# Moving a head's gate and its norm's last product from GpSimd to VectorE, read out of PSUM

## The chip, the cores and the metric

One core of one Trainium2 chip runs the whole model. The metric is the device time of one execution in microseconds; lower is better. The engines' names are those of the profile: PE is TensorE's matmuls (PEld its weight loads), DVE VectorE, ACT ScalarE, POOL GpSimd, SP SyncE, which here only issues DMAs.

## The reference

Two layers on 1024 rows of width 1024: an S5 layer, then a layer of differential attention with 8 heads, then a final norm. The change lies in the second layer:

```python
q, z = jnp.split(xn @ in_w, [QK_WIDTH], axis=-1)
...
o = diff_attention(q1, q2, k1, k2, v, lam)
o = rmsnorm(o, subln_g, SUBLN_EPS) * (1.0 - lam_init)
o = o.reshape(bsz, seq, ATTN_WIDTH) * jax.nn.silu(z)
return o @ out_w
```

Each head has 128 value columns. Its mixture o is normalized over these 128 (the gains are folded into weights) and multiplied by the gate silu(z). All products on TensorE are made from a high and a low part of one or both operands (three matmuls, lines 159 to 161).

## The kernel before

The S5 layer takes the first 485 us or so and is not touched. `layer1` walks over 32 steps: 8 heads, 4 blocks of 256 queries each, in falling order for odd heads. Everything lies transposed: 128 value columns on the partitions, 256 queries along the free axis. One step consists of

- `scores`: TensorE's products of k and q into a bank `s` (840, 841; the second multiplies a zero-padded tile `z00` to `z11`, which holds the high part of q for one of the two maps), VectorE's masked minimum (846), ACT's exponentials (848), and the difference of the two softmaxes (856);
- `turn`: TensorE transposes it into a bank `t` (874), ACT and VectorE split it into `ph` and `pl` (876, 877);
- `mix`: TensorE sums v times these into another bank `t` (890 to 892). ACT copies the bank to `ob` (896) and squares it twice (897, 898), GpSimd takes the low part of the squares (899);
- `head_norm`, one step later: two products with a matrix of ones add the squares over the partitions into a bank `t` (907, 908); ACT takes Ln and Exp (909, 910: the inverse root), into the tile `sq`; SP loads the gate `zt` from `zg` in HBM (913); GpSimd multiplies `ob` by `zt` (914) and by `sq` (915); the result goes to HBM (917), or for the last head into `oh` and `ol` by ACT and VectorE (919, 920).

The pool of the banks `t` has two buffers, shared by `turn`, `mix` and `head_norm`. TensorE's filler between the steps of one head are the projections of the next head's k, q, gate and v (`PLAN`): a head's q (lines 766 to 787) is rotated by VectorE (`xr`), cast by ACT into the padded tile (782, 783) and brought to `q` by SP (784, 785). At the last head the filler is the output projection of the first 512 columns (`out1`), and then `final`, which does the rest in four pieces of 256 columns. Their weights are loaded by SP into `mraw` (745) and split by ACT (`mhi` or `vh`, 749) and VectorE (`mlo` or `vl`, 750). The first weight that `final` loads into its own pool lies in memory that the attention layer's tiles give back, so its load waits for their last readers.

No order is written out for these engines: a list scheduler puts each engine's instructions into one fixed order, from its own costs, when the kernel is built. Each engine then runs its list in order and waits at an instruction for what that one needs. So a change of a few lines can move instructions in the whole layer.

Of the kernel before, what the change touches and what calls it, by code (L numbers as in the profile page):

```python
# [8 lines left out]
F32 = mybir.dt.float32  # L9
# [3 lines left out]
AF = mybir.ActivationFunctionType  # L13
# [5 lines left out]
P = 128  # L19
# [31 lines left out]
def rd(ap):  # L51
    return ap.bitcast(F32)


class Trunk:
# [822 lines left out]
            out.append((ph, pl))  # L878
        return out

    def mix(self, pt, v, qb):

        mm = self.nc.tensor.matmul
        o = self.pst.tile([P, 512], F32, name="t")
        nj = 2 * qb + 2
        for j in range(nj):
            c0 = 1 if j == nj - 1 else 0
            ov = o[:, c0 * P:2 * P]
            ph, pl = (t[:, j % 2, c0:2, :].rearrange("p a b -> p (a b)") for t in pt[j // 2])
            mm(ov, v[0][:, j, :], ph, start=j == 0, stop=False)  # L890
            mm(ov, v[0][:, j, :], pl, start=False, stop=False)  # L891
            mm(ov, v[1][:, j, :], ph, start=False, stop=j == nj - 1)  # L892
        ob = self.op.tile([P, 256], F32, name="ob")
        sq = self.op.tile([P, 256], F32, name="sq", bufs=1)
        sh, sl = (self.op.tile([P, 256], F32R, name=f"sq{x}", bufs=1) for x in "hl")
        self.nc.scalar.copy(ob, o[:, 0:256])
        self.nc.scalar.activation(sq, o[:, 0:256], AF.Square)
        self.nc.scalar.activation(sh, o[:, 0:256], AF.Square)
        self.nc.gpsimd.tensor_sub(sl, sq, rd(sh))
        return ob, sq, sh, sl  # L900

    def head_norm(self, ob, sq, sh, sl, zg, dst, qb):

        nc = self.nc
        V, S = nc.vector, nc.scalar
        ss = self.pst.tile([P, 512], F32, name="t")
        nc.tensor.matmul(ss[:, 0:256], self.onesr.broadcast_to([P, P]), sh, start=True, stop=False)
        nc.tensor.matmul(ss[:, 0:256], self.onesr.broadcast_to([P, P]), sl, start=False, stop=True)
        S.activation(sq, ss[:, 0:256], AF.Ln, bias=self.small1[:, 2:3], scale=1.0 / P)
        S.activation(sq, sq, AF.Exp, scale=-0.5)  # L910
        qs = slice(qb * 256, qb * 256 + 256)
        zt = self.op.tile([P, 256], F32, name="zt", bufs=1)
        nc.sync.dma_start(zt, zg[:, qs])
        nc.gpsimd.tensor_mul(ob, ob, zt)
        nc.gpsimd.tensor_mul(ob, ob, sq)  # L915
        if len(dst) == 1:
            nc.sync.dma_start(dst[0][:, qs], ob)
        else:
            S.copy(dst[0][:, qs], ob)
            V.tensor_sub(dst[1][:, qs], ob, rd(dst[0][:, qs]))  # L920

    def layer1(self, dbg=None):
        tc, nc, I = self.tc, self.nc, self.I
        V, G, S = nc.vector, nc.gpsimd, nc.scalar
        zg = [self.dr.tile([P, SEQ], F32, name="zg") for _ in range(NH)]
        og = [self.dr.tile([P, SEQ], F32, name="og") for _ in range(NH)]
        self.close_mm()
        with ExitStack() as es:
            pool = lambda n, b, **k: es.enter_context(tc.tile_pool(name=n, bufs=b, reuse_waits="tile", **k))
            rp = self.rp.enter_context(tc.tile_pool(name="rope", bufs=1, reuse_waits="tile"))  # L930
            self.RC = rp.tile([P, SEQ], F32, name="RC")
            self.RS = rp.tile([P, SEQ], F32, name="RS")
            self.xs = [rp.tile([P, 512], F32, name=f"xs{i}") for i in range(2)]
            nc.sync.dma_start(self.RC, I["rc"])
            nc.sync.dma_start(self.RS, I["rs"])
            for c in (0, 512):
                cs = slice(c, c + 512)
                V.tensor_mul(self.RC[:, cs], self.RC[:, cs], self.R1[:, cs])
                G.tensor_mul(self.RS[:, cs], self.RS[:, cs], self.R1[:, cs])
            for x in self.xs:  # L940
                G.memset(x, 0.0)
            self.vp = self.rp.enter_context(tc.tile_pool(name="vp", bufs=3, reuse_waits="tile"))
            self.tq, self.st, self.qp = pool("tq", 2), pool("st", 2), pool("qp", 2)
            zp = pool("zp", 1)
            self.padded = [[zp.tile([P, 512], F32R, name=f"z{i}{j}") for j in range(2)] for i in range(2)]
            for z in self.padded:
                for x in z:
                    G.memset(x.bitcast(F32), 0.0)
            self.ep, self.pp, self.op, self.tiny = pool("ep", 2), pool("pp", 4), pool("op", 2), pool("tiny", 4)
            self.pst, self.pss = pool("pst", 2, space=PSUM), pool("pss", 2, space=PSUM)  # L950
            self.psm = self.rp.enter_context(tc.tile_pool(name="psm", bufs=2, space=PSUM, side="right",
                                                          reuse_waits="tile"))
            vs, kq = {}, {}

            units = {
                "k": lambda h: kq.setdefault(h, []).append(self.project_kq(h, I["kv_w"], self.sm("gkv"), "k")),
                "q": lambda h: kq[h].append(self.project_kq(h, I["b_in_w"], self.gq, "q")),
                "v": lambda h: vs.update(zip((h, h + 1), self.project_v(h // 2))) if h % 2 == 0 else None,
                "g": lambda h: self.gate(h, zg[h]),
            }  # L960
            wv = self.load_v(0)
            wk = self.load_early(I["kv_w"], 0, self.sm("gkv"))
            vs.update(zip((0, 1), self.project_v(0, wv)))
            kq[0] = [self.project_kq(0, I["kv_w"], None, "k", wk)]
            units["q"](0)
            steps = [(h, 3 - qb if h in DESCENDING else qb) for h in range(NH) for qb in range(4)]
            nxt = self.scores(*kq[0], steps[0][1])
            self.gate(0, zg[0])
            norm = None
            for n, (h, qb) in enumerate(steps):  # L970
                cur = nxt
                if n + 1 < len(steps):
                    hn, qn = steps[n + 1]
                    nxt = self.scores(*kq[hn], qn)
                if h + 1 < NH:
                    for u in PLAN[n % 4]:
                        units[u](h + 1)
                pt = self.turn(cur, qb)
                if norm:
                    self.head_norm(*norm)  # L980
                if (h, n % 4) == (NH - 1, 0):
                    oh, ol = ([self.act(f"{x}{k}") for k in range(KT)] for x in ("oh", "ol"))
                    for k in range(NH - 1):
                        self.gated(og[k], EARLY, oh[k], ol[k])
                dst = (og[h],) if h < NH - 1 else (oh[h], ol[h])
                norm = (*self.mix(pt, vs[h], qb), zg[h], dst, qb)
            self.head_norm(*norm)
            parts = self.out1(og, oh, ol)
        self.final(oh, ol, *parts)
        self.rp.close()  # L990
# [188 lines left out]
```

## Time and profile before

| | us |
| --- | --- |
| runs, median (lowest to highest of 3) | 1091.48 (1090.79 to 1091.61) |
| profiled execution | 1093.5 |
| its span | 1091.7 |
| PE busy | 1061.9 |
| DVE busy | 822.5 |
| ACT busy | 623.9 |
| POOL busy | 235.3 |

The span is what the profiler recorded from the first instruction to the last; the execution's own time is a little longer. Busy time of an engine is the time in which one of its instructions ran. Times in a trace are microseconds from the start of the span.

### The profile page before, as it was taken

To read this page: it belongs to the slowest core of one execution; us is meant where nothing else is said; L and a number is where in the kernel's file an instruction comes from. 1 tells how busy PE (TensorE), PEld (TensorE's weight loads), DVE (VectorE), ACT (ScalarE), POOL (GpSimd) and SP (SyncE) were. 2 spreads that over 40 slices of the span, in tenths; PEclk is the share of its full clock that TensorE was granted. 3 is DMA by queue.
4 is the path that set the end of the run, shared out by engine and by line. 5 is a ranking of instruction groups with operands and counts; after the bars stand their busy time and mean duration, and the time that the engine had idled before them with its cause. 6 is when DMAs were issued, how large, how long until landed. Compare 5 with 4: busy or idle time off the path is not lost. (4 is left out here: it accounts for less than half of the span.)

```text
span 1091.7 us, 17715 instructions
## 1 busy us (share of the span) xinstructions
PE 1061.9 (97%) x6308; PEld 908.2 (83%) x6308; DVE 822.5 (75%) x1617; ACT 623.9 (57%) x1396; POOL 235.3 (22%) x237
## 2 busy tenths in 40 slices
PE   7999999999999999999999999999999999899996
PEld 5678888887788888998888898889988898788896
DVE  7789999984577543547898778877698777987475
ACT  6432343332534332436787788767788778785463
POOL 0000000000356112211222122221222222210258
PEclk9999999999899999999999999999999999999998
DMA  8143546544654445313122212222222222553344
GB/s 283 45 136 116 174 151 174 159 151 133 238 193 135 127 140 157 135 42 90 44 85 57 73 56 66 86 56 78 66 53 79 60 84 61 148 175 105 109 134 159
DMA packets 143143, 125.94 MB, mean 115 GB/s; under 512 B 9808, under 2 KB 123216, under 8 KB 143056
## 3 DMA queue, kind: packets, MB, share of 16 engines
q1 hardware_dynamic: 134736, 120.63, 36.0%
q10 hardware_dynamic: 8320, 4.19, 1.3%
q8 instruction: 49, 0.80, 0.3%
q14 instruction: 38, 0.31, 0.1%
HBM read 85.48 MB, written 33.03 MB: 109 GB/s over the span
## 5 line engine op out<-in xcount | busy, mean ns | idle before, releaser
L159 PE MATMUL pm<-h1h,mhi 128*128 128x512 f32 x352 | 139.5, 396 | 1.0 <-DVE xr L767 1.0
L160 PE MATMUL pm<-h1l,mhi 128*128 128x512 f32 x352 | 138.8, 394 | 0.0
L161 PE MATMUL pm<-h1h,mlo 128*128 128x512 f32 x352 | 138.6, 394 | 0.0
L848 ACT ACTIVATE e<-e,tiny 128x256 f32<-128x256 f32 (+7 forms) x128 | 99.3, 777 | 33.6 <-DVE tiny L846 32.5
L846 DVE CUSTOM_DVE_ANT_0 e<-s,tri 128x256 f32<-128x256 f32 (+7 forms) x128 | 94.8, 750 | 11.9 <-PE s L841 6.3
L750 DVE TENSOR_TENSOR mlo<-mraw,mhi 128x1024 fp32r<-128x1024 f32 (+1 forms) x44 | 59.9, 1360 | 42.7 <-ACT mhi L749 42.5
L749 ACT CAST mhi<-mraw 128x1024 fp32r<-128x1024 f32 (+1 forms) x44 | 45.3, 1030 | 76.0 <-PE ps L160 55.0
L159 PE MATMUL ps<-xh,mhi 128*128 128x512 f32 x208 | 82.2, 395 | 1.9 <-DVE evo L491 1.9
L161 PE MATMUL ps<-xh,mlo 128*128 128x512 f32 x208 | 81.9, 394 | 0.0
L160 PE MATMUL ps<-xl,mhi 128*128 128x512 f32 x208 | 81.7, 393 | 0.0
L159 PEld LDWEIGHTS pm<-h1h,mhi 128*128 128x128 f32 x352 | 66.2, 188 | 14.7 <-DVE xr L767 2.4
L161 PEld LDWEIGHTS pm<-h1h,mlo 128*128 128x128 f32 x352 | 66.2, 188 | 12.7
L771 POOL TENSOR_TENSOR xs<-xs,RS 128x512 f32<-128x512 f32 x32 | 42.9, 1340 | 156.0 <-DMA xs<-ze 114.2
L160 PEld LDWEIGHTS pm<-h1l,mhi 128*128 128x128 f32 x352 | 66.2, 188 | 12.2
L840 PE MATMUL s<-k,q 128*128 128x384 f32 (+4 forms) x192 | 67.9, 356 | 3.0 <-DMA q<-z 3.0
L915 POOL TENSOR_TENSOR ob<-ob,sq 128x256 f32<-128x256 f32 x32 | 25.7, 803 | 190.3 <-ACT sq L910 177.9
L841 PE MATMUL s<-k,z 128*128 128x384 f32 (+4 forms) x192 | 65.9, 346 | 0.0
L810 PE MATMUL pm<-mhi,h1h 128*128 128x256 f32 x224 | 64.5, 288 | 1.1 <-DVE z L698 0.8
L735 ACT ACTIVATE mhi<-mraw,small 128x128 fp32r<-128x128 f32 (+1 forms) x152 | 51.8, 414 | 21.5 <-PE ps L160 14.4
L811 PE MATMUL pm<-mlo,h1h 128*128 128x256 f32 x224 | 63.3, 284 | 0.1
L812 PE MATMUL pm<-mhi,h1l 128*128 128x256 f32 x224 | 63.1, 283 | 0.0
L877 DVE TENSOR_TENSOR pl<-t,ph 128x512 fp32r<-128x512 f32 (+2 forms) x112 | 54.9, 492 | 10.8 <-ACT ph L876 10.4
(375 smaller groups left out, 3091.0 us busy)
## 6 DMA issues: line engine op xcount, KB each, us to landing
mraw<-in_kv_w SPq DMA_DIRECT2D x16, 512.0 KB
mraw<-in_b_in_w SPq DMA_DIRECT2D x16, 512.0 KB
mraw<-in_in_w SPq DMA_DIRECT2D x13, 512.0 KB
ud<-evo SPq DMA_DIRECT2D x16, 256.0 KB
ug<-ud SPq DMA_DIRECT2D x8, 512.0 KB
kd<-ks SPq DMA_DIRECT2D x8, 512.0 KB
toep<-kd SPq DMA_DIRECT2D x8, 512.0 KB
yd<-yb ACTq DMA_DIRECT2D x8, 512.0 KB
```

The costliest lines, as they stand in the source:

```text
L159: mm(ps, wh, xh, start=first, stop=False)
L160: mm(ps, wh, xl, start=False, stop=False)
L161: mm(ps, wl, xh, start=False, stop=last)
L750: nc.vector.tensor_sub(lo, raw, rd(hi))
L810: mm(o, self.h1h[k][:, ts], wh, start=k == 0, stop=False)
L811: mm(o, self.h1h[k][:, ts], wl, start=False, stop=False)
L812: mm(o, self.h1l[k][:, ts], wh, start=False, stop=k == KT - 1)
L840: mm(sps[m][:, c, :w], q2[m][:, qt], ks[m][:, cs], start=True, stop=False)
L841: mm(sps[m][:, c, :w], q2[2 + m][:, qt], ks[m][:, cs], start=False, stop=True)
L846: V.tensor_tensor_reduce(out=blocks(em[:, :L]), in0=sp[:, 0:nb, :w], in1=blocks(self.tri[:, SEQ - L:]), scale=-1.0, scalar=3e38, op0=ALU.a ...
L848: S.activation(em[:, :L], em[:, :L], AF.Exp, bias=nmx[:, m:m + 1], scale=-1.0, accum_out=sm[:, m:m + 1])
L877: V.tensor_sub(pl[:, jj, ii, :], tp[:, jj, ii, :], rd(ph[:, jj, ii, :]))
```

## The change

`mix` loads the gate itself and VectorE multiplies the bank by it, in place of ACT's copy. In `head_norm` ACT writes Ln and Exp back into the bank, and VectorE multiplies `ob` by the bank. Both GpSimd products are gone; GpSimd keeps the low part of the squares. The squares are taken of the mixture without the gate, as before.

```diff
-        self.nc.scalar.copy(ob, o[:, 0:256])
+        zt = self.op.tile([P, 256], F32, name="zt", bufs=1)
+        self.nc.sync.dma_start(zt, zg[:, qb * 256:qb * 256 + 256])
+        self.nc.vector.tensor_mul(ob, o[:, 0:256], zt)
         self.nc.scalar.activation(sq, o[:, 0:256], AF.Square)
         self.nc.scalar.activation(sh, o[:, 0:256], AF.Square)
         self.nc.gpsimd.tensor_sub(sl, sq, rd(sh))
-        return ob, sq, sh, sl
+        return ob, sh, sl
...
-        S.activation(sq, ss[:, 0:256], AF.Ln, bias=self.small1[:, 2:3], scale=1.0 / P)
-        S.activation(sq, sq, AF.Exp, scale=-0.5)
+        S.activation(ss[:, 0:256], ss[:, 0:256], AF.Ln, bias=self.small1[:, 2:3], scale=1.0 / P)
+        S.activation(ss[:, 0:256], ss[:, 0:256], AF.Exp, scale=-0.5)
         qs = slice(qb * 256, qb * 256 + 256)
-        zt = self.op.tile([P, 256], F32, name="zt", bufs=1)
-        nc.sync.dma_start(zt, zg[:, qs])
-        nc.gpsimd.tensor_mul(ob, ob, zt)
-        nc.gpsimd.tensor_mul(ob, ob, sq)
+        V.tensor_mul(ob, ob, ss[:, 0:256])
```

In the changed kernel the gate's load is line 897, VectorE's products are 898 and 914, ACT's squares 899 and 900, the sums 909 and 910, Ln and Exp 911 and 912; from 915 on a line has the number before, less one.

The scheduler's order changes with it from the second head on. Three places follow, with the numbers of the tiles and what an instruction waits for; the words in brackets are the engines or DMA queues it waits for.

First ACT, at the cast of the last head's q into the padded tile (`z10`), before:

```order
L876 CAST ph_9747<-t_9746 128x512 [waits PE_49]
L782 CAST z10_3845<-xr_9719 64x512 [waits DVE_49]
L783 CAST z11_3846<-xr_9719 64x512
L700 ACTIVATE ze_9892<-ze_9892 128x512 [waits DMAHW3_49,DMAHW4_49,DMAHW2_49,DMAHW5_49,DVE_49,Activation_49]
```

and now:

```order
L749 CAST mhi_10416<-mraw_10418 128x896 [waits DMAHW4_49,PE_49]
L876 CAST ph_9525<-t_9524 128x128 [waits DVE_49]
L782 CAST z10_3845<-xr_9696 64x512 [waits PE_49]
L783 CAST z11_3846<-xr_9696 64x512 [waits PE_49]
L848 ACTIVATE e01_9597,tiny_9586<-e01_9597,tiny_9586 128x1024 [waits DVE_49]
```

The cast waited for the rotated q of VectorE; now it waits for TensorE, whose last product with the tile's former contents stands here, 20 instructions ahead of the first one with the new (`q0_9706`):

```order
L841 MATMUL s_9587<-k0_8532,z10_3845 128x512
L840 MATMUL s_9588<-k1_8533,q1_8831 128x512 [waits DVE_49]
...
L874 MATMUL t_9714<-ident_67,e00_9382 128x128
L874 MATMUL t_9714<-ident_67,e01_9404 128x128
L840 MATMUL s_9779<-k0_9415,q0_9706 128x448 [waits DMAHW6_49,DVE_49,PE_49]
L841 MATMUL s_9779<-k0_9415,z10_3845 128x448 [waits Activation_49]
```

Second TensorE from the last transposes (`t_10371` before, `t_10343` now) to the first product with the first weight that `final` loads itself (`mhi_10776` before, `mhi_10744` now). Before:

```order
L892 MATMUL t_10350<-ph_10330,vl_9058 128x128
L874 MATMUL t_10371<-ident_67,e00_10291 128x128 [waits PE_49]
L874 MATMUL t_10371<-ident_67,e01_10309 128x128 x2
L161 MATMUL pm_10699<-oh2_10107,mlo_10665 128x512
...
L161 MATMUL pf_10825<-oh7_10112,vl_10743 128x256
L159 MATMUL pf_10857<-oh0_10105,mhi_10776 128x256 [waits Activation_49]
L160 MATMUL pf_10857<-ol0_10113,mhi_10776 128x256
L161 MATMUL pf_10857<-oh0_10105,mlo_10777 128x256 [waits DVE_49]
```

and now:

```order
L874 MATMUL t_10343<-ident_67,e00_10264 128x128 [waits DVE_49]
L874 MATMUL t_10343<-ident_67,e01_10282 128x128 x2
L159 MATMUL pm_10666<-oh7_10084,mhi_10626 128x512 [waits Activation_49]
...
L909 MATMUL t_10353<-sqh_10335,onesr_70 128x256 [waits PE_49,Activation_49]
L890 MATMUL t_10361<-ph_10344,vh_9036 128x256 [waits DVE_49,PE_49]
...
L910 MATMUL t_10353<-sql_10336,onesr_70 128x256 [waits Pool_49]
L159 MATMUL pf_10825<-oh0_10077,mhi_10744 128x256 [waits Activation_49]
L160 MATMUL pf_10825<-ol0_10085,mhi_10744 128x256
L909 MATMUL t_10378<-sqh_10370,onesr_70 128x256 [waits PE_49,Activation_49]
L161 MATMUL pf_10825<-oh0_10077,mlo_10745 128x256 [waits DVE_49]
```

Between the transposes and that weight stood 51 instructions, 19 of them with 512 columns; now it is 17: six with 512 columns, eight with 256 and three with 128. The transposes' bank, freed by ACT before, is now freed by VectorE.

Third SP's list at the same place, before:

```order
L745 DMA mraw_10744<-in_b_out_w 128x8x128 [waits DMAHW4_49,DVE_49]
L745 DMA mraw_10778<-in_b_out_w 128x8x128 [waits DMAHW7_49,PE_49]
L745 DMA mraw_10784<-in_b_out_w 128x8x128
L913 DMA zt_10412<-zg_3801 128x256 [waits DMAHW5_49,Pool_49]
L1053 DMA fh256_10814<-h1d_3271 128x256
```

and now:

```order
L745 DMA mraw_10712<-in_b_out_w 128x8x128 [waits DMAHW3_49,DVE_49]
L897 DMA zt_10337<-zg_3801 128x256 [waits DMAHW4_49,DVE_49]
L745 DMA mraw_10746<-in_b_out_w 128x8x128 [waits PE_49]
L897 DMA zt_10372<-zg_3801 128x256 [waits DMAHW6_49,DVE_49]
L745 DMA mraw_10752<-in_b_out_w 128x8x128 [waits Activation_49]
```

The two weights' loads followed each other; now a gate's load and a wait for ACT stand between them, and the first still waits for the transposes.

## Rows read from the trace of the kernel before

**Rows 1.** The page's part 1, busy us, share of the span and instructions of each engine.
```profile
PE 1061.9 (97%) x6308; PEld 908.2 (83%) x6308; DVE 822.5 (75%) x1617; ACT 623.9 (57%) x1396; POOL 235.3 (22%) x237
```

**Rows 2.** The table by stages: us, then busy us of each engine, granted clock.
```profile
core 0: us, PE busy (x) PEld busy (x) DVE busy (x) ACT busy (x) POOL busy (x), PEclk, DMA share, GB/s
530.00:600.00 70.00, 70.00 (x364) 59.05 (x364) 63.23 (x138) 55.16 (x120) 16.48 (x16) 1.00 0.25 70
...
930.00:985.00 55.00, 50.03 (x258) 42.37 (x257) 49.45 (x92) 44.26 (x86) 11.79 (x12) 0.96 0.53 163
```

**Rows 3.** PE's waits, 930 to 985: us in total, times, longest.
```profile
PE s L840 <- DMA q<-z: 3.0, 1, 3.0
PE pm L161 <- DVE mlo L750: 0.8, 1, 0.8
PE t L874 <- ACT sqh L898: 0.6, 1, 0.6
```

**Rows 4.** PE's timeline: start, us, line, out<-in; two pairs of neighbours.
```profile
957.47 0.42 PE L891 MATMUL t<-pl,vh 128*128 128x256 f32 x1
957.68 0.42 PE L892 MATMUL t<-ph,vl 128*128 128x256 f32 x1
...
987.34 0.39 PE L161 MATMUL pm<-oh,mlo 128*128 128x512 f32 x1
987.57 0.39 PE L159 MATMUL pm<-oh,mhi 128*128 128x512 f32 x1
```

**Rows 5.** Groups by shape, 530 to 1055: count, busy us, mean ns, idle before.
```profile
L914 POOL TENSOR_TENSOR ob<-ob,zt 128x256 f32<-128x256 f32 x32 | 29.3, 916 | 107.0 <-ACT ob L896 86.9 <-PE t L874 14.3 <-PE pm L161 5.7
L915 POOL TENSOR_TENSOR ob<-ob,sq 128x256 f32<-128x256 f32 x32 | 25.7, 803 | 190.3 <-ACT sq L910 177.9 <-ACT ph L876 6.5 <-DVE pl L877 5.9
...
L909 ACT ACTIVATE sq<-t,small 128x256 f32<-128x256 f32 x32 | 14.9, 466 | 1.3 <-PE t L908 1.2
...
L910 ACT ACTIVATE sq<-sq 128x256 f32<-128x256 f32 x32 | 13.3, 415 | 0.3
L877 DVE TENSOR_TENSOR pl<-t,ph 128x256 fp32r<-128x256 f32 x31 | 12.9, 417 | 1.9 <-ACT ph L876 1.8
...
L896 ACT COPY ob<-t 128x256 f32<-128x256 f32 x32 | 11.7, 365 | 4.7 <-PE t L892 4.2
```

**Rows 6.** DVE groups of the same stretch; last row: L772's min/median/max ns.
```profile
L772 DVE TENSOR_TENSOR xr<-xr,xs 128x512 f32<-128x512 f32 x27 | 20.8, 771 | 11.7 <-POOL xs L771 11.6
L736 DVE SCALAR_TENSOR_TENSOR mlo<-mraw,small,mhi 128x128 fp32r<-128x128 f32 x96 | 31.7, 380 | 2.4 <-ACT mhi L735 2.1
L736 DVE SCALAR_TENSOR_TENSOR mlo<-mraw,gq,mhi 128x128 fp32r<-128x128 f32 x48 | 14.0, 346 | 2.8 <-ACT mhi L735 2.8
...
L772 DVE TENSOR_TENSOR xr<-xr,xs x32: 672/692/1211, 491.1 to 948.4; 128x512 f32<-128x512 f32 x32
```

**Rows 7.** Timelines of ACT and PE; idle time before a row stands in brackets.
```profile
949.14 0.62 ACT L782 CAST z<-xr 64x512 fp32r<-64x512 f32 x1 [2.34 <-DVE xr L772]
...
955.08 0.44 PE L840 MATMUL s<-k,q 128*128 128x448 f32 x1 [3.00 <-DMA q<-z]
```

**Rows 8.** The same path for an earlier head: ACT, then PE.
```profile
620.37 0.62 ACT L782 CAST z<-xr 64x512 fp32r<-64x512 f32 x1
...
623.36 0.28 PE L908 MATMUL t<-sql,onesr 128*128 128x256 f32 x1
623.48 0.28 PE L840 MATMUL s<-k,q 128*128 128x256 f32 x1
```

**Rows 9.** The tail: SP's waits, 1020 to 1055, then timelines of PE, ACT, DVE.
```profile
SPq L745 <- PE t L874: 4.9, 1, 4.9
...
1031.81 0.30 PE L874 MATMUL t<-ident,e 128*128 128x128 f32 x1
1040.25 0.28 PE L159 MATMUL pf<-oh,mhi 128*128 128x256 f32 x1
...
1036.23 1.05 ACT L749 CAST mhi<-mraw 128x1024 fp32r<-128x1024 f32 x1 [2.26 <-DMA mraw<-in_b_out_w]
...
1037.31 1.23 DVE L750 TENSOR_TENSOR mlo<-mraw,mhi 128x1024 fp32r<-128x1024 f32 x1 [3.02 <-ACT mhi L749]
```

More of the change, by code (lines that the diff above doesn't have):

```diff
@@ L879, in turn, with mix @@
         return out
-    def mix(self, pt, v, qb):
+    def mix(self, pt, v, qb, zg):
         mm = self.nc.tensor.matmul
@@ L899, in mix, with head_norm @@
         self.nc.gpsimd.tensor_sub(sl, sq, rd(sh))
-        return ob, sq, sh, sl
-    def head_norm(self, ob, sq, sh, sl, zg, dst, qb):
+        return ob, sh, sl
+    def head_norm(self, ob, sh, sl, dst, qb):
         nc = self.nc
@@ L985, in layer1 @@
                 dst = (og[h],) if h < NH - 1 else (oh[h], ol[h])
-                norm = (*self.mix(pt, vs[h], qb), zg[h], dst, qb)
+                norm = (*self.mix(pt, vs[h], qb, zg[h]), dst, qb)
             self.head_norm(*norm)
```

## The prediction, made before the changed kernel ran

> **What bounds the kernel now.** The profiled execution took 1093.5 us for a span of 1091.7, so 1.8 lie around the span, and it is 2.0 above the median of the runs, 1091.48. Sums below are made against 1093.5 and carried over to the median as differences. Some 0.2% (2.2 us) is what a measurement of this kernel can tell from no change.
>
> I read the page's totals first: TensorE is busy 97% of the span, VectorE 75%, GpSimd 22% [rows 1]. So a gain must come from TensorE's few gaps, and a loss from new ones. The table by stages, over the attention layer (485 to 1055 us), shows where the gaps are: none at 530 to 600, 5 of 55 us at 930 to 985 [rows 2]. VectorE is busy 63 of 70 us in the one and 49 of 55 in the other, 90% each; that counts for the change, which adds to VectorE. The list of waits for 930 to 985 names the gaps: 3.0 us for the load of head 7's q, 0.8 for a weight's lower half, 0.6 for transposes that stand behind the bank of the mixture [rows 3]. The timeline adds what the longest costs beyond the wait: up to 959.6 the mixture's products of 256 columns come every 0.21 us [rows 4], where 0.12 is their pace elsewhere [rows 8]. A doubled pitch is the lower of the clock's two levels, 1.2 GHz for 2.4, and the granted clock of that stage is 0.96 [rows 2]. From 956.2, where it begins, that is 3.4 us at half the pace, 1.7 lost.
>
> **The change, part by part.** There are 32 steps (8 heads, 4 blocks of queries); each counts once.
>
> ACT's copy out of the bank goes: 32 by 365 ns, 11.7 us. Both of GpSimd's products go: 29.3 and 25.7 us. VectorE gains 64 products of 128x256 with one operand in PSUM; the nearest row is its subtraction of that size and source, 417 ns, so 64 by 0.417 = 26.7 us [rows 5]. None of the waits of TensorE that I read ends on the removed operations, so the removal itself brings nothing but relief for other engines.
>
> Relief of VectorE: two of its lines have means above what an undisturbed one takes, L772 771 against its median 692, L736 380 against 346 in its other form of that size; the surplus is 27 by 0.08 and 96 by 0.034, 5.4 us [rows 6]. If GpSimd's 123 operations of the layer (32 at each of its three lines of a step, 27 ahead of L772) carry it alike, the removed 64 give back 2.8 us; lines whose surplus I don't see would add to that, up to the 4.5 I allow. VectorE's net is then +22 to +24 us over 525, where it has some 100 us free. The Trainium skill (SBUF — State Buffer, "SBUF: two separate sides") says that a GpSimd operation and a VectorE one with two SBUF inputs lock each other out for a whole instruction. By that rule L772's maximum would be one such collision, and the 64 new products, with one input in PSUM, would meet none; no row here shows the latter.
>
> How long a bank is held: the sum's bank was free after one Ln of 466 ns; now Ln, Exp (415) and VectorE's product (417) follow on each other, 1.3 us plus hand-offs, for which I take 0.1 each: 1.6. The mixture's bank was held 1.1 us by three ACT reads of the copy's size (365 each [rows 5]); now VectorE reads first and ACT's squares wait for it, so 1.15 us plus VectorE's queue. There are two such banks, so the second tile after this one waits. With TensorE's pitch (0.12 us for 256 columns [rows 8], 0.23 for 512 [rows 4], half of 0.23 for a transpose) over the order of its instructions, the work between a sum and that tile is 3.7 to 13 us in the new order before the last two steps, and behind a mixture 2.0 us or more where 0.9 was the least. So I cost the longer hold at nothing there. The cover is that work; where it is gone, each step would cost up to 1.6 us. The 0.6 us at 981 was the 0.9 us place [rows 3], and goes: -0.6.
>
> The load of head 7's q: the 3.0 us wait [rows 3] began with the rotated q, late at 949.1 (2.34 us idle before the cast, until VectorE's xr), and ended with the first use at 955.08: 5.9 us from the cast's start [rows 7]. In the new order xr has 18.3 us of work to hide behind where it had 13.6, enough for the 16.6 of before. But the padded tile z10 that the cast fills is now read last by TensorE only 2.6 us ahead of that first use (20 before): in the order above the cast waits for PE. The same path at 620, with the queue free, took from the cast's start at 620.37 to a use without a wait at 623.48, 3.1 us [rows 8]. So the wait becomes 0.5 to 3.3 us. I take 1.7, towards neither end, since two stores and two loads now stand ahead: -1.3. If all of the wait and its slow stretch went, it would be -4.7; the other end is +0.3.
>
> The tail: the filler that stood between the last mixtures is used up earlier. The last transposes now wait for VectorE's product with the sum's bank: hold 1.6 us, work behind it 1.3, +0.3. More follows. The raw tile of the first weight that the final stage loads itself (454 on SP in both orders) lies where the last transposes read, and is released by them: SP waits 4.9 us for that now [rows 9]. From the transposes at 1031.81 the cast starts 4.4 us later, at 1036.23, and ends at 1037.28; the lower half ends at 1038.54. TensorE wants them at 1040.25, 8.4 us after the transposes began, so 3.0 and 1.9 us are to spare. In the new order the transposes and what follows take 0.3 + 6 by 0.23 + 8 by 0.12 + 3 by 0.08 = 2.9 us. The first product then waits 5.5 - 2.9, some 2.5 us, and two further on the lower half, 1.26 us later, costs 1.0; the sum of squares between them, behind that cast in ACT's queue, ends no later. The second such weight was loaded at once with the first; now a zt load and a wait for ACT stand between, so 0 to 2 us more, taken as 1.0. A low clock after these waits, 0 to 1.7 us as at 956, is not in the sum but in the range.
>
> Sum: -0.6 - 1.3 + 0.3 + 2.5 + 1.0 + 1.0 = +2.9, so 1096.4 for such an execution and **1094.4 us** for the median.
>
> **The rivals.**
> - *The closing stalls go, the tail is milder.* q lands in time (-4.7 with the slow stretch), the bank is free (-0.6), and the late weight costs only its 2.5 less some 1.0 that the transposes and the tiles ahead of it, late themselves, cover: -3.8, 1087.7 us. For it speaks xr's larger cover; against, z10's late release. Chance 0.22.
> - *It cancels.* q gains 2.5 (its path at the short end), the bank 0.6, and the tail costs the 3.5 of the first weight alone: +0.4, 1091.9 us. Chance 0.20.
> - *VectorE's queue becomes the bound.* Its new products stand in order: one that waits for Exp, or for a mixture, holds back softmax behind it, and ACT's squares and exponentials behind those. The place is where VectorE is 90% busy, 530 to 600 and 930 to 985 [rows 2], 125 of 525 us; their part of 23 us is 5.5, on top of the sum: +8.4, 1099.9 us. It decides once the queue adds more than the 2 to 3.7 us of work that covers a bank. Chance 0.13. The Trainium skill (PSUM — Partial Sum Buffer, "PSUM bank collisions raise a hardware error") says that two engines may not read one bank and quadrant at once and that nothing stalls them, so the program must order them. By that rule ACT's square can't start beside VectorE's product, and ACT inherits VectorE's lateness; the new order, in which the square waits for DVE, agrees, while no run of before shows the price.
>
> That the change doesn't do what it says is excluded by the order: both products stand in VectorE's list.
>
> **How the numbers follow.** The forecast has 0.45, the rivals 0.22, 0.20 and 0.13. Faster by over 0.2% (below 1089.3): the first rival and 0.03 of the second, 0.25. Same: the rest of the second and 0.05 of the forecast's low end (below 1093.7), 0.22. Slower: the rest of the forecast and the third rival, 0.53. The forecast's own range is 1092 to 1097.5 (second weight 0 to 2, slow clock 0 to 1.7, q -2.5 to +0.3). The range asked for reaches down to the first rival and up to the third: 1087.0 to 1100.0.
>
> **What would show it.** After: ACT without the copy, GpSimd near 235 - 55 = 180 us, VectorE near 845. At 930 to 985 a shorter wait for q and no wait of transposes for the squares. Around the last mixtures TensorE waits for a cast of the final's first weight, then for its lower half, 3 us and more in one place, and SP's chain shows that load right behind the transposes. I am wrong if TensorE stays full between the last transposes and the final's first product, if VectorE's means for the new products are far from 417 ns, or if waits for VectorE's products appear in the middle of the layer.

## The result and the profile after

The changed kernel takes 1100.49 us (median of 4 runs, 1098.99 to 1101.36), the kernel before 1091.55 beside it (4 runs): ratio 1.0069, 95% interval 1.0052 to 1.0085, so 7.5 us slower by the ratio (the medians are 8.9 apart). By the ratio that is 1099.0 for the 1091.48 that the forecast was made against; the forecast was slower by 2.9, and its range reached to 1100.0. Sign and main place were right; the size was not. The profiled execution took 1100.75 us for a span of 1098.7, 7.0 above the span before.

The page's totals after, to hold against [rows 1]:

```profile
PE 1062.5 (97%) x6308; PEld 909.0 (83%) x6308; DVE 835.4 (76%) x1681; ACT 616.3 (56%) x1364; POOL 177.4 (16%) x173
```

GpSimd lost 58 us, VectorE gained only 13, and TensorE is as busy as before in a longer span. The table by stages (busy us of PE, PEld, DVE, ACT, POOL, then the granted clock) says where, beside [rows 2]:

```profile
core 0: us, PE busy (x) PEld busy (x) DVE busy (x) ACT busy (x) POOL busy (x), PEclk, DMA share, GB/s
530.00:600.00 70.00, 69.70 (x358) 59.27 (x357) 64.21 (x145) 55.43 (x118) 10.48 (x9) 1.00 0.25 69
930.00:985.00 55.00, 48.59 (x241) 39.58 (x240) 49.88 (x100) 43.86 (x85) 5.01 (x5) 0.97 0.52 161
1020.00:1055.00 35.00, 31.87 (x208) 29.16 (x207) 18.85 (x42) 18.16 (x44) 2.33 (x3) 0.95 0.44 128
```

And the row of the last of these stages in the kernel before:

```profile
1020.00:1055.00 35.00, 35.00 (x239) 32.41 (x239) 17.50 (x26) 18.16 (x39) 12.05 (x15) 1.00 0.51 151
```

At 530 to 600, where VectorE is 92% busy now, TensorE lost 0.3 us. At 1020 to 1055 it was full and is now 3.1 us idle, at a clock of 0.95. I added up, over TensorE's matmuls, how much later each neighbour starts than at the usual pitch (the time from one start to the next) of its size. Against before, in one trace of each, that is 0.2 us more up to 485, 1.7 less at 530 to 930, 0.8 more at 930 to 990, 5.4 more at 1025 to 1062, 0.7 more from there to the last product of weights, which starts 5.9 us later; these sum to 5.4, and missing matmul records leave 0.5 open. From there to the end it is 12.7 us for 11.6, another 1.1.

TensorE's waits from 485 on, in the trace after (us in total, times, longest), of which [rows 3] showed one stage before:

```profile
PE ps L1068 <- ACT fsq L1058: 3.0, 1, 3.0
PE pf L159 <- ACT mhi L749: 2.1, 1, 2.1
PE pm L161 <- DVE mlo L750: 2.1, 1, 2.1
PE s L840 <- DVE tiny L846: 1.9, 3, 0.8
PE t L891 <- DVE pl L877: 1.6, 1, 1.6
PE pm L160 <- DVE ol L996: 1.2, 1, 1.2
```

By its name the load of head 7's q is gone from the list; 0.7 us of waiting for it is left under another name (below). Four of these six end on VectorE; the first two are the very end and the tail. The tail's pieces in the timelines of PE and ACT (start, duration, idle time before in brackets), beside [rows 9]:

```profile
1037.73 0.30 PE L874 MATMUL t<-ident,e 128*128 128x128 f32 x1
...
1040.60 0.33 PE L910 MATMUL t<-sql,onesr 128*128 128x256 f32 x1
1043.08 0.39 PE L159 MATMUL pf<-oh,mhi 128*128 128x256 f32 x1 [2.14 <-ACT mhi L749]
...
1044.00 0.39 PE L909 MATMUL t<-sqh,onesr 128*128 128x256 f32 x1 [0.42 <-ACT sqh L900]
...
1046.34 0.41 PE L159 MATMUL pf<-oh,mhi 128*128 128x256 f32 x1
1046.55 0.41 PE L160 MATMUL pf<-ol,mhi 128*128 128x256 f32 x1
```

```profile
1041.98 1.04 ACT L749 CAST mhi<-mraw 128x1024 fp32r<-128x1024 f32 x1 [2.56 <-DMA mraw<-in_b_out_w]
```

From the last transposes to the cast's start it is 4.25 us (4.4 before), from these to the product that needs it only 5.35, 2.1 of it waiting, where 8.4 us of work stood. From 1045.5 to 1048.9 the products come every 0.21 us, TensorE's lower clock level, though it had waited last at 1044.

The end, DVE and then ACT and PE:

```profile
1087.91 0.94 DVE L1085 SCALAR_TENSOR_TENSOR xs<-xs,small,R 128x256 f32<-128x256 f32 x1
1088.77 0.41 DVE L1053 TENSOR_TENSOR h<-pf,fh 128x256 f32<-128x256 f32 x1
```

```profile
1089.28 0.42 ACT L1058 ACTIVATE fsq<-h 128x256 f32<-128x256 f32 x1 [3.82 <-DVE h L1053]
```

```profile
1089.75 1.10 PE L1068 MATMUL ps<-fsq,small 128*128 128x256 f32 x2 [3.01 <-ACT fsq L1058]
```

The last residual (L1053) now stands on VectorE behind four products that scale the piece before it; TensorE's last sum of squares waits for it. In the trace before it stood ahead of them:

```profile
1080.38 0.42 DVE L1054 TENSOR_TENSOR h<-pf,fh 128x256 f32<-128x256 f32 x1 [1.97 <-PE pf L161]
1081.23 1.05 DVE L1086 SCALAR_TENSOR_TENSOR RC<-RC,small,R 128x256 f32<-128x256 f32 x1 [0.42 <-ACT R L679]
```

The four products take 3.3 to 3.6 us either way, and the final scaling of the last piece waits behind them before, so the difference at the end is 1.1 and not 3.

At 940 to 956 most of what stands in the place of q's wait is VectorE's queue. DVE, then PE:

```profile
949.99 1.08 DVE L750 TENSOR_TENSOR mlo<-mraw,mhi 128x896 fp32r<-128x896 f32 x1
950.99 0.28 DVE L877 TENSOR_TENSOR pl<-t,ph 128x128 fp32r<-128x128 f32 x1
951.19 0.67 DVE L786 TENSOR_TENSOR q<-xr,z 64x512 fp32r<-64x512 f32 x1
```

```profile
951.33 0.33 PE L891 MATMUL t<-pl,vh 128*128 128x128 f32 x1 [1.55 <-DVE pl L877]
...
952.89 0.44 PE L840 MATMUL s<-k,q 128*128 128x448 f32 x1 [0.67 <-DVE tiny L851]
```

The mixture waits for the low half of a transposed tile that stands behind a weight's lower half. The 0.67 us ahead of q's first use is put down to a reciprocal of VectorE (L851) that this product doesn't read. VectorE's own part of q (L786) had ended at 951.86, and in the trace the last of 16 signals that the load of q landed stands at 952.76, so that wait is what is left of the load's.

The lower clock is the other difference of this stage. Before, it stood twice, for 3.4 us each, from 956.2 and from 983.5; the forecast read the first alone. After it stands once, from 953.4. The rows of 980 to 990, before and then after:

```profile
980.00:990.00 10.00, 8.35 (x33) 6.16 (x32) 8.69 (x15) 5.54 (x12) 1.43 (x2) 0.83 0.29 88
980.00:990.00 10.00, 10.00 (x51) 8.54 (x50) 7.87 (x18) 6.16 (x14) 0.00 (x0) 1.00 0.41 126
```

TensorE's waits of 930 to 990 rose from 5.0 to 6.4 us, and one slow stretch less gave back some 1.7.

The new operations cost what was expected, in the groups by shape of 530 to 1055:

```profile
L898 DVE TENSOR_TENSOR ob<-t,zt 128x256 f32<-128x256 f32 x32 | 13.3, 417 | 3.7 <-DMA zt<-zg 2.8 <-PE t L892 0.5
L914 DVE TENSOR_TENSOR ob<-ob,t 128x256 f32<-128x256 f32 x32 | 13.2, 413 | 1.6 <-ACT t L912 1.2
...
L899 ACT ACTIVATE sq<-t 128x256 f32<-128x256 f32 x32 | 12.1, 379 | 10.1 <-DVE ob L898 6.3 <-DVE tiny L851 3.4 <-DVE tiny L854 0.2
```

ACT stood idle 6.3 us in all for VectorE's product ahead of its square, and no TensorE wait in the list of 530 to 930 ends on such a square.

### The profile page after: what moved, and what is told of

Same layout as the page of the kernel before. It is cut to its first block, busy times and chain, and to the rows that moved or that the text cites. A ratio compares the mean times of both kernels' runs of the same rounds, so it can differ in the third digit from the quotient of the medians.

```text
span 1098.7 us, 17655 instructions
## 1 busy us (share of the span) xinstructions
PE 1062.5 (97%) x6308; PEld 909.0 (83%) x6308; DVE 835.4 (76%) x1681; ACT 616.3 (56%) x1364; POOL 177.4 (16%) x173
## 4 chain that ended last, share of the span: by engine, by line
PE 62%; DVE 23%; ACT 5%; DMA 5%; issue 4%; SPq 1%; POOL 0%; DVEq 0%; ACTq 0%; POOLq 0%
PE ps L159 7%; PE ps L160 7%; PE ps L161 7%; PE pm L159 6%; PE pm L161 6%; PE pm L160 6%; DVE w L310 5%; PE pm L810 2%; PE pm L811 2%; PE pm L812 2%; PE t L874 2%; PE s L841 2%; PE s L840 2%; DVE mlo L736 2%; DMA mraw<-in_b_in_w 2%
## 5 line engine op out<-in xcount | busy, mean ns | idle before, releaser
L159 PE MATMUL pm<-h1h,mhi 128*128 128x512 f32 x352 | 138.9, 395 | 0.9 <-DVE xr L767 0.9
L750 DVE TENSOR_TENSOR mlo<-mraw,mhi 128x1024 fp32r<-128x1024 f32 (+1 forms) x44 | 57.0, 1294 | 37.9 <-ACT mhi L749 37.9
L159 PE MATMUL ps<-xh,mhi 128*128 128x512 f32 x208 | 82.2, 395 | 1.9 <-DVE evo L491 1.9
L159 PEld LDWEIGHTS pm<-h1h,mhi 128*128 128x128 f32 x352 | 66.2, 188 | 13.5 <-DVE xr L767 1.8
L901 POOL TENSOR_TENSOR sql<-sq,sqh 128x256 fp32r<-128x256 f32 x32 | 26.0, 811 | 311.1 <-ACT sqh L900 293.5
```

The lines of the kernel that those rows point to most:

```text
L159: mm(ps, wh, xh, start=first, stop=False)
L750: nc.vector.tensor_sub(lo, raw, rd(hi))
```

## The experiments

The theory (A): the loss comes from where the fixed order now puts instructions (the last transposes close to the final's first weight, the end, the waits for VectorE at 940 to 985). The rival (B): VectorE's added work and the longer hold of the banks cost it directly.

**Gate alone.** The change without its second half; Ln and Exp go to SBUF and GpSimd multiplies by the root.

```diff
-        V.tensor_mul(ob, ob, ss[:, 0:256])
+        nc.gpsimd.tensor_mul(ob, ob, sq)
```

> Only the gate's product is moved to VectorE and the mixture's bank; the root stays in SBUF and on GpSimd. Theory A (the loss of some 9 us comes from where instructions now stand: too little work between the last transposes and the first weight of the final stage, and four products ahead of the last residual on VectorE at the very end): in this order 6.6 us of work stand in the first place (2.5 in the change, 8.0 before), so the wait for the weight is under 0.5 us, and only the end's order is the change's: 1091.5 to 1094. Theory B (VectorE's new work and the longer hold of the banks cost it directly): half of the operations, half of the loss, near 1096.

Measured 1.0015 (1.0004 to 1.0027), +1.6 us. TensorE's list of waits from 485 on has none for the final's first weight; the end's is there:

```profile
PE ps L1068 <- ACT fsq L1058: 3.0, 1, 3.0
PE t L909 <- DVE pl L877: 2.3, 2, 2.1
```

As A expected, for the tail and in total. The total is a balance, though: 1.5 us at 1019, where transposes wait for ACT's Ln (`PE t L874 <- ACT sq L911`), stand against 3.9 less than before at 530 to 930, and A names neither.

**Root alone.** ACT's copy, the gate's load and GpSimd's product with it stay.

```diff
-        nc.gpsimd.tensor_mul(ob, ob, sq)
+        V.tensor_mul(ob, ob, ss[:, 0:256])
```

> Only the root stays in its bank and is multiplied by VectorE; the gate stays on GpSimd and ACT's copy stays. Theory A: 7.3 us of work after the last transposes and the order of before at the end, so no loss: 1090 to 1092.5. Theory B: the sum's bank is held 1.6 us in place of 0.5 in every step, half of the loss or more: 1095 to 1097.

Measured 1.0047 (1.0029 to 1.0064), +5.1 us: B's number, but not in B's places. The tail and the end are as before; the time goes at 530 to 930, 7.7 us more by TensorE's pitches, in waits like these (that stage):

```profile
PE pm L810 <- DVE vl L817: 2.3, 2, 1.7
PE pm L810 <- DVE z L698: 1.5, 1, 1.5
PE t L890 <- DVE pl L877: 1.3, 1, 1.3
...
PE t L874 <- DVE ob L915: 0.4, 1, 0.4
```

Only the last ends on the new product, 0.4 us; the others end on older operations of VectorE. The longest, 1.7, stood behind other work in its queue; but VectorE itself had sat idle 1.55 us for a store of the gate (`zg<-z`) ahead of the 1.5, and 0.37 for ACT ahead of the 1.3. At 930 to 990 this kernel loses 4.7 less than the one before, so its total is a balance too. The whole change, with twice the new work on VectorE, has no such losses at 530 to 930. So A failed on this kernel's total, and B on where it went: a late VectorE can decide in the middle, but the amount of work doesn't say when.

**Head 7 as before.** The change for heads 0 to 6; the last head takes the old functions.

```diff
+                if h < NH - 1:
+                    norm = (self.head_norm, *self.mix(pt, vs[h], qb, zg[h]), dst, qb)
+                else:
+                    norm = (self.head_norm_old, *self.mix_old(pt, vs[h], qb), zg[h], dst, qb)
```

> The change for heads 0 to 6; head 7 is done as before (ACT's copy, two GpSimd products). Its order has the change's place for the last transposes (2.5 us of work ahead of the first final weight) and the change's end. Theory A: the same time as the change within 1.5 us, 1099 to 1102, with the wait of 2 us for the cast still there. Theory B: the tail's loss is made by VectorE's products in head 7 itself and goes, 1094 to 1096.

Measured 1.0067 (1.0049 to 1.0085), the change's 1.0069. None of head 7's steps makes the new products, and the waits of TensorE are there all the same:

```profile
PE ps L1112 <- ACT fsq L1102: 3.0, 1, 3.0
PE pf L159 <- ACT mhi L749: 2.2, 1, 2.2
PE pm L161 <- DVE mlo L750: 2.1, 1, 2.1
PE t L891 <- DVE pl L877: 1.5, 1, 1.5
```

This settles the tail and the end for A, against new work in head 7 itself: they are a matter of the order that the change of the earlier heads leaves behind.

**The end's order.** The last four products issued behind the last residual, everything else as in the change.

```diff
-                    V.tensor_add(t, pt, h1)
+                    added = V.tensor_add(t, pt, h1)
...
+                if last:
+                    with tc.issue_after(added.ins):
+                        self.scale_out(*before)
```

> The change, with the four products that scale the third piece issued behind the last residual on VectorE. Theory A: TensorE's wait of 3.0 us for the last squares falls to some 0.3 as before; the scaling of the last piece waits for the four products instead, as before, so 1.0 to 1.5 us are gained: 1099 to 1099.5. A rival: the wait was the whole difference at the end, 3 us gained: 1097.5. If neither, the end's order costs nothing: 1100.5.

Measured 1.0046 (1.0028 to 1.0063), 2.5 us less than the change, though the intervals overlap. In its trace TensorE waits 0.5 us there, and from the last product of weights to the end it takes 10.9 us in place of 12.7, so 1.9 of the 2.5 lie there. The gain is between the 1.0 to 1.5 of A and the 3 of its rival.

**The fourth weight early**, in the change and in the kernel before, and **the lower halves on GpSimd**, alone and together with the first and the end's order.

```diff
-        w.append(self.load_m(I["b_out_w"], 0, KT, 2 * P, P, slots=(self.vp, ("vh", "vl"))))
+        for m in (2, 3):
+            w.append(self.load_m(I["b_out_w"], 0, KT, m * P, P, slots=(self.vp, ("vh", "vl"))))
```

```diff
-        nc.vector.tensor_sub(ol[:, hs], raw, rd(oh[:, hs]))
+        nc.gpsimd.tensor_sub(ol[:, hs], raw, rd(oh[:, hs]))
```

> The change, and the fourth weight of the output projection is loaded and split as the third one is, through the raw tile and into the pool of v's parts, so that it waits for no memory that the last transposes read; the order then also has the last residual ahead of the four products at the end, as before. Theory A (the late release of the first weight of the final stage makes the tail's loss): the wait for that cast (2.1 us), the one for its lower half and the stretch at the lower clock behind them go, 4 to 6 us, and 2.5 at the end as when that was done alone: 1092.5 to 1094.5. Rival: the filler is short whatever weight comes when, and TensorE waits for the mixtures' chain instead: only the end's 2.5 are gained, 1097 to 1098.

> The kernel before, with the fourth weight loaded through the pool of v's parts. Before, its cast ended 3.0 us ahead of its use, so by theory A nothing is gained: within 0.1% of before. A gain of 2 us or more would mean that the edit helps of itself, and would take from what the same edit shows in the change.

Measured 1.0069 (1.0055 to 1.0082) for the change with it, and 1.0053 (1.0036 to 1.0069) for the kernel before with it: a clear miss, of the rival too. In the change the wait for the weight's cast goes, but others come in both kernels: in the change 2.9 us for the last head's result (`pf L159 <- ACT oh L918`), in the kernel before 2.2 for a low half, in the tail of a kernel that had none:

```profile
PE t L890 <- DVE pl L877: 2.2, 1, 2.2
```

The edit re-orders the tail and is no clean test of the weight. What it shows is that the tail of before was not robust either: an edit that changes no amount of work, only where one weight lies, cost it 5.8 us.

> The change, with the lower half of the gated mixtures for the output projection (14 subtractions of 128x512 at the last head) on GpSimd, where the change made room, in place of VectorE. Theory: at 940 to 985 VectorE (90 to 95% busy in the trace of the change) is what TensorE waits for, in three places of 1.2 to 2.1 us; without some 10 us of subtractions there the stage gains 2 to 4 us: 1096.5 to 1098.5. Rival: the waits there are for chains (a load, a cast, then VectorE), not for its queue, or GpSimd is too late with the halves: no gain, 1100 to 1102.

Measured 1.0066 (1.0053 to 1.0078): no gain that stands out from the noise. The wait for `mlo` goes; others change their names (1.0 us for GpSimd's halves, 1.0 for a cast), and the one for `pl`, 1.5, stays.

> The change with three edits at once: the last products behind the last residual, the fourth weight through the pool of v's parts, the lower halves on GpSimd. If the three losses (end 2.5, tail 4 to 6, VectorE's queue at 940 to 985 2 to 4) are separate ones, they add up: 1088 to 1092, at or below the kernel before. If they are one loss that moves on, it stays above 1094.

Measured 1.0044 (1.0032 to 1.0057), above 1094: no more than the end's order alone brought. The losses don't add up; one moves on into the next (here 2.7 us for the cast of a weight that lies with v's parts).

**The filler held back.** The change with the end's order, and the products of the third weight in the first piece issued by TensorE behind the last transposes.

```diff
+                    with tc.issue_after(self.turned) if c0 == PIECES[0][0] and m in (2,) else ExitStack():
+                        for k in range(k0, KT):
+                            self.mm3(pt, w[m][0][:, k, :], w[m][1][:, k, :], oh[k][:, cs], ol[k][:, cs],
+                                     k == k0, k == KT - 1)
```

> The change, the end's order mended (last products behind the last residual), and the 24 products of the third weight in the first piece issued by TensorE behind the last transposes, not ahead of them: 5.0 us of the same work then stand between these and the first weight of the final stage, in place of 2.5. Theory A (the wait for that weight is set by how much of TensorE's work stands there): that wait falls from 2.2 to about 0.4 us, the slow clock behind it goes, some 0.6 us of new waits come ahead of the transposes, so 2.5 to 4 us less than with the end alone (1.0046): ratio 1.001 to 1.0025. Rival (the loss moves on, as with the fourth weight): TensorE waits as long for the mixtures' chain ahead of the transposes: ratio 1.004 to 1.005.

Measured 1.0037 (1.0023 to 1.0051), between A's range and the rival's, and not distinct from the 1.0046 of the end's order alone. The cast's wait is gone, as A expected of 5 us of work in that place. These stand there now (TensorE's waits, then the row of 1025 to 1062, with the end's order alone and in this run):

```profile
PE t L909 <- DVE pl L877: 1.1, 1, 1.1
PE t L890 <- DVE pl L877: 0.5, 1, 0.5
PE pf L161 <- DVE mlo L750: 0.4, 1, 0.4
```

```profile
1025.00:1062.00 37.00, 32.77 (x246) 30.60 (x244) 20.18 (x44) 19.36 (x46) 8.17 (x10) 1.00 0.43 125
1025.00:1062.00 37.00, 34.85 (x252) 32.96 (x251) 21.18 (x46) 19.63 (x49) 8.97 (x11) 0.95 0.42 125
```

TensorE waits 2.1 us less there, but in this trace the clock fell, which it had not in the other, so only 1.0 came back by the pitches. The mechanism held, most of its price did not come back. What TensorE still waits for there are mostly the mixtures' low halves, ahead of the work that was moved; that these are the next limit was not tested.

**The square first.** As the last, and ACT's squares before VectorE's product in the bank.

```diff
-        self.nc.vector.tensor_mul(ob, o[:, 0:256], zt)
         self.nc.scalar.activation(sq, o[:, 0:256], AF.Square)
         self.nc.scalar.activation(sh, o[:, 0:256], AF.Square)
+        self.nc.vector.tensor_mul(ob, o[:, 0:256], zt)
```

> As the run before it in this list, and in each mixture's bank ACT's squares stand first and VectorE's product with the gate last: the same instructions in another order. It gives other places all over the layer; the padded tile of head 7's q is now read last 11.9 us ahead of its new use (2.6 in the change). If the waits at 940 to 985 come from where things stand, that stage changes by 1 us or more either way, and the time is within 2 us of the run before it; if they come from VectorE's amount of work, the stage stays as it was.

Measured 1.0018 (1.0007 to 1.0029), 2 us less. At 930 to 990 its pitches lose 8.6 us where the run before it lost 12.3: the waits there depend on places. Now q's load is waited for longer (2.2 us for 0.2), and 3.5 us more are lost at 530 to 930.

**Gate alone, mended**, with the end's order, and the same with the square first.

> Only the gate's product is moved (ratio 1.0015 alone), with the last products behind the last residual, which brought 2.5 us in the whole change. If the end's loss is separate from the rest: ratio 0.999 to 0.9995, at or just below the kernel before. If not: 1.0015.

> As the run before it, with ACT's squares first in the bank and VectorE's product last. 11.8 us of work stand between the last transposes and the first weight of the final stage (6.6 in the run before it, 8.0 before). The amounts of work on each engine are the same, so a difference of 2 us or more between the two shows what the order alone can do; by the amounts of work there is none: ratio 0.999 to 1.0005.

Measured 0.9997 (0.9985 to 1.0008) and 1.0059 (1.0040 to 1.0078). The first came out as the end's loss alone would have it (0.9997 for 1.0015) and is the best version found; it is not distinct from the kernel before, and no version beats that one. The second is the plainest result of the study: the same instructions in another order, 6.8 us slower by the ratios. At 530 to 930 TensorE waits in the first for

```profile
PE t L874 <- ACT sqh L900: 0.4, 1, 0.4
PE t L909 <- DVE pl L877: 0.2, 1, 0.2
PE pm L159 <- DVE xr L767: 0.2, 1, 0.2
```

and in the second for

```profile
PE s L840 <- DVE tiny L846: 1.8, 3, 0.9
PE t L909 <- DVE pl L877: 1.1, 2, 0.7
PE pm L810 <- DVE vl L817: 0.7, 1, 0.7
```

and 5.4 us more are lost there by pitches. B's "by the amounts of work there is none" is refuted.

## Why the prediction was right in sign and short in size

- *Cost of the operations.* Right: 417 and 413 ns for 417 forecast, none of the 64 over 425; GpSimd 177.4 for 180.
- *Relief of VectorE.* Mis-sized: 2.8 to 4.5 us were forecast, but VectorE's total rose by 12.9 with 26.5 added, so 13.6 came back. L772 of [rows 6] gave 1.6 of it, its mean being 713 ns now for 771; L736, the other line that was read, kept its mean (385 ns for 380), and the weights' lower halves (L750), which were not read, gave 2.9. How much comes back varies with the order: the gate alone has 2.5 and 9.8 us more than before in its two mended orders, for 13.3 added. Which operations meet was not tried apart.
- *Bank holds cost nothing in the middle.* Right for the whole change: no wait for a sum's bank stands in the list of 530 to 930, and the pitches there lose 1.7 us less than before. Where this gain comes from was not tested.
- *The bank wait at 981* went, as forecast.
- *The load of q, "-1.3".* The wait for the load itself came out shorter than taken, 0.7 us for 1.7 (issue at 949.93, use at 952.89). The step that failed is that the stage's sum put VectorE's queue at nothing: TensorE waits 1.6 us for it just ahead of q's use, and 1.2 and 2.1 behind it, where 0.8 stood before. So the stage lost 0.8 where 1.9 were to be won with the bank, and it would have lost more but for the slow stretch at 983.5 that went. The forecast looked at the load's own path and not at what stood ahead of TensorE's other instructions. The third rival had the engine right, for this stage and not for 530 to 600. That its 1099.9 lies close to what was measured is luck: its 5.5 us were to come from both stages, and the tail's clock and the end were not in it.
- *The tail.* Right in mechanism, nearly in size, and there with luck. The first weight's wait was 2.1 us of idle and 2.35 of pitch for 2.5; the next 0.4 to 0.8, by the sum of squares and not the lower half, for 1.0; 0.6 to 0.7 ahead of the mixture, for a low half and not for the bank, for 0.3; the second weight cost nothing for 1.0; and the slow clock, which stood only in the range, cost 1.4 (15 products by 0.09) in this trace. Together +5.4 for 4.8. With the end's order alone a wait of 2.2 us stood in the same place and no slow clock followed.
- *The end* was no term at all. The forecast followed the new order to the second weight and took what follows as it was. It cost 1.1 us against before in the trace, and 2 to 2.5 came back in two kernels when the order there was mended (1.9 and 2.0 of it at the end, by their traces).
- *The cancelling rival and the faster one* fell: the tail's loss came whole, and what q gained was taken by VectorE.
- That VectorE's added work is the cause was refuted for the tail (head 7 as before) and as a general account (the pair of equal work). That no order could make the change pay is not shown: with three edits it came to 1.0018, and half of it to 0.9997.

## What to carry to other kernels

When a scheduler fixes the order, a small edit in the middle re-orders what comes after it, and on a kernel whose TensorE is 97% busy that can cost more than the edit was to bring: walk the new order to its last instruction, the end of the program included. For each wait that you expect to go, look at what stands ahead of the waiting instruction on its own engine and on the engines that feed it, since a neighbour's wait can take its place. Before a result is put down to the operations moved, run the same operations in a second order: here that alone was worth 6.8 us.

## What the runs showed of the hardware

- The lower clock level can come after the wait and not with it: in the change TensorE waited last at 1044.0, ran 8 products at 0.12 us, and only at 1045.5 the pitch rose, for 15 at 0.21. Before, the wait ended at 955.08 and the pitch doubled from 956.2. It doesn't follow each wait: behind the change's 2.1 us that ended at 978.39 TensorE kept its full pace, and so it did behind the 2.2 us of the tail with the end's order alone (granted clock 1.00 at 1025 to 1062). What a wait costs beyond itself could not be told from its length here.
- Ln and Exp in place in the bank are shorter than with SBUF as target: Ln 440 ns for 466, Exp, whose source was in SBUF too, 372 for 415 (440 and 376 with the root alone). The groups of 530 to 1055 after:

```profile
L911 ACT ACTIVATE t<-t,small 128x256 f32<-128x256 f32 x32 | 14.1, 440 | 1.8 <-PE t L910 1.7
...
L912 ACT ACTIVATE t<-t 128x256 f32<-128x256 f32 x32 | 11.9, 372 | 0.4
```
